# A transformer layer on one core: scaling of the second tokens on VectorE, low parts of the output projection on VectorE, first projections by bank

## The chip, the cores and the metric

The kernel runs on one core of a Trainium2 chip. The metric is the device time of one execution in microseconds (us), the median of several runs. TensorE multiplies matrices into PSUM banks, ScalarE, VectorE and GpSimd do the elementwise work, and SyncE issues the DMAs. Each of them works through its own queue in order; semaphores order them against each other.

## What is computed

One layer of an encoder over 2048 tokens of width 1024. What matters here is its first half:

```python
h = x * (1.0 + sc1) + sh1                       # sc1, sh1: a vector each, from c
proj = jnp.einsum('bsd,de->bse', h, w_in[l])    # u (512), q, k, v (512 each)
y_pool = pool_mixer(u, w_pool[l], pool_scale[l])
y_attn = chunked_attention(q, k, v, rel_bias[l])     # 8 heads, 9 chunks of 64 keys
y = jnp.einsum('bse,ed->bsd', jnp.concatenate([y_pool, y_attn], axis=-1), w_out[l])
x = layer_norm(ALPHA * x + (1.0 + g1) * y, ln1_g[l], ln1_b[l])
```

A squared-ReLU MLP (1024 to 4096 and back) and a second layer norm follow; no line of the change is in them.

## The kernel before

**Two parts per operand.** Each operand of a large product is kept as a high part (the value rounded to the matrix type, a copy on ScalarE) and a low part (value minus high part, a subtraction on VectorE or GpSimd). A product is three matmuls per 128 rows of the contraction: high by high, high by low, low by high. `split` (lines 57 to 59) issues the copy and the subtraction; its last argument is the engine of the subtraction.

**Stages.** The tokens go in two halves of 1024. The operand `hT` (128 partitions, high and low, 8 contraction blocks, 1024 tokens) lies in one buffer, which serves three things in turn: `h` of the first tokens, `h` of the second tokens, the output projection's weights.

- *Start* (to about 57 us): for each of 8 contraction blocks `k`, `chain0` and `fold0` make the two modulation vectors, `fold0` and `low0` make `hT` of that block, and `dense0(k)` (line 161) issues 18 matmuls: 3 passes by 3 projections (`FIRST`: A0 is q and k of head 0, V0 the values of heads 0 and 1, U0 a pooling group) by 2 halves of 512 tokens. They accumulate in six PSUM banks: A0 in the wide tile `S`, V0 in two of the three `d` banks, U0 in the third and in `pv`. The weights lie in the pool `ada`, which ends after this stage; the pool `attn` takes its place.
- *Attention with the other projections under it* (about 57 to 672 us): the loop over `units` (2 halves, 8 heads, 8 blocks of 128 queries) issues per unit `scores` (TensorE into `S`, line 600; VectorE adds the bias and takes the extremum, 607; ScalarE exponentiates, 609), `normalise` (VectorE reciprocal 614, GpSimd scaling 615), `transposes` (TensorE into `T`, 623), `probs` (ScalarE 631 and VectorE 632 out of `T`), and for every second unit `values` and `combine`. `S` and `T` have one buffer each. Between them `step` (line 446) lets the generator `dense` issue one projection matmul at a time, and calls `finish_evacs`, which moves each projection's evacuation (`evac`) on by one piece: ScalarE and VectorE take `q`, `k` or values out of their bank, values are transposed by TensorE (line 318).
- *Side work.* After every sixth matmul (every third for `wo_pieces(1)`) `dense` moves a side generator on by one piece. `h_pieces(tb)` (line 253) makes `h` of 512 second tokens, in 8 pieces: call `k` issues the scaling of piece `k` (GpSimd, 267), the high part of piece `k-1` (ScalarE, 269), the low part of piece `k-2` (VectorE, 271), and then a load. It runs twice, during the last blocks on the first tokens and the first block group on the second. `wo_pieces(n)` (line 663) does the like with the output projection's weights: load, copy, subtraction, eight pieces, twice. Both draw their raw tiles from `xr` (`xr_tile`, line 248), a ring of 4 buffers that the generator `extras` uses too: it loads `wout` (517), scales it on GpSimd (527) and stores it. `extras` pauses from unit 44 to unit 70 (line 727).

**The order around the change.** It is written out by hand (`manual_schedule`): each engine executes its instructions in the order in which Python issues them. The order of `pend` (line 362), from which `finish_evacs` takes one piece of each kind per call, is that of `FIRST`: A0, V0, U0. Weights of the projections are split by `split` on GpSimd (`hl`, line 59).

Of the kernel before, what the change touches and what calls it, by code (L numbers as in the profile page):

```python
# [11 lines left out]
ALU = mybir.AluOpType  # L12
# [12 lines left out]
def trunk_layer(ctx: ExitStack, tc: tile.TileContext, xT, x, wada1, wada2, vecs, rows, win, wfirst, wpT, wout,  # L25
                bias, w1, w2, out):
    nc = tc.nc
# [25 lines left out]
    mod1 = const.tile([128, 8, 2], F32, name="mod1")  # L53
# [3 lines left out]
    def split(hl_h, hl_l, src, low):  # L57
        nc.scalar.copy(hl_h, src)  # L58
        low.tensor_sub(hl_l, src, hl_h.bitcast(F32))  # L59
# [43 lines left out]
    FIRST = ("A0", "V0", "U0")  # L103
# [14 lines left out]
    hT = big.tile([128, 2, 8, 1024], F32R, name="hT", tag="big")  # L118
# [15 lines left out]
    def dbank():  # L134
        return pp.tile([128, 512], F32, name="d", tag="d", bufs=3)
# [4 lines left out]
    def narrow(w=512):  # L140
        return pr.tile([128, w], F32, name="pv", tag="pv", bufs=1)
# [3 lines left out]
    NF0 = len(FIRST)  # L145
    wf = ada.tile([128, 2, 8, NF0, 128], F32R, name="wf")
    s0 = wide("S")
    first = {(0, 0): s0[:, 0:512], (0, 1): s0[:, 512:1024], (1, 0): dbank(), (1, 1): dbank(), (2, 0): dbank(),
             (2, 1): narrow()}
# [9 lines left out]
        ld[k] = (wr, wa, xk)  # L159

    def dense0(k):
        for i, (a, b) in enumerate(((0, 0), (1, 0), (0, 1))):
            for c in range(NF0):
                for tb in range(2):
                    nc.tensor.matmul(first[c, tb], wf[:, a, k, c, :], hT[:, b, k, tb * 512:tb * 512 + 512],
                                     start=(k == 0 and i == 0), stop=(k == 7 and i == 2))

    acs = {}

# [36 lines left out]
    for k in range(8):  # L206
        if k < 4:
            load0(k + 4)
        if k == 4:
            st.dma_to(1)  # L210
        if k < 7:
            fold0(k + 1)
        if k < 6:
            chain0(k + 2)
        if k < 7:
            low0(k + 1)
        if k < 6:
            split0(k + 2)
        if k == 5:
            st.split_to(1)  # L220
        dense0(k)
# [20 lines left out]
    def flush():  # L242
        while later:
            later.pop(0)[1]()
# [3 lines left out]
    def xr_tile():  # L248
        while stores:
            stores.pop(0)()  # L250
        return ap.tile([128, 512], F32, name="xr", tag="xr", bufs=4)

    def h_pieces(tb):
        c0, cols = 1024 + tb * 512, slice(tb * 512, tb * 512 + 512)
        rs = {}

        def load(k):
            rs[k] = xr_tile()
            nc.sync.dma_start(rs[k], xT[k, :, c0:c0 + 512])

        for k in range(4):
            load(k)
        yield
        for k in range(10):
            if k < 8:
                r = rs[k]
                nc.gpsimd.tensor_scalar(r, r, mod1[:, k, 1:2], mod1[:, k, 0:1], op0=ALU.mult, op1=ALU.add)
            if 1 <= k < 9:
                nc.scalar.copy(hT[:, 0, k - 1, cols], rs[k - 1])
            if k >= 2:  # L270
                nc.vector.tensor_sub(hT[:, 1, k - 2, cols], rs.pop(k - 2), hT[:, 0, k - 2, cols].bitcast(F32))
                if k + 2 < 8:
                    load(k + 2)
            if k < 7 or k == 9:
                yield
# [3 lines left out]
    def alloc(hf, kind, idx):  # L279
        if kind == "A":  # L280
            Qt[hf, idx] = ap.tile([128, 1024], F32R, name="q", bufs=2)
            Kt[hf, idx] = kk = ap.tile([128, 2, 1536], F32R, name="k", bufs=2)
            if hf:
                for s in range(2):
                    nc.sync.dma_start(kk[64 * s:64 * s + 64, :, 0:512].bitcast(F32), kS[idx].bitcast(F32))
        elif kind == "V":
            Vt[hf, idx] = vv = ap.tile([128, 12, 2, 128], F32R, name="v", bufs=2)
            if hf:
                nc.sync.dma_start(vv[:, 0:4].bitcast(F32), vS[idx].bitcast(F32))
# [61 lines left out]
    def run(g):  # L351
        for _ in g:
            pass
# [4 lines left out]
    def both(c, name):  # L358
        for tb in range(2):
            yield from evac(0, name[0], int(name[1]), tb, first[c, tb], dbank)  # L360

    for c, name in enumerate(FIRST):
        alloc(0, name[0], int(name[1]))
        g = both(c, name)
        pend.append((g, (0, name), name[0]))
# [30 lines left out]
    def dense():  # L396
        w, open_, side = {}, [], iter(())
        for hf, name, tb in blocks():
# [11 lines left out]
            if (hf, name, tb) in ((0, "U1", 1), (1, "A0", 0), (1, "A0", 1), (1, "U0", 1)):  # L410
                run(side)
                side = iter(()) if (hf, name, tb) == (1, "A0", 1) else wo_pieces(0) if (hf, name) == (1, "U0") else h_pieces(hf)
                next(side, None)
# [15 lines left out]
            pend.append((evac(hf, kind, idx, tb, ps, dbank), (hf, name) if tb else None, kind))  # L429
        run(side)  # L430
        side = wo_pieces(1)
        next(side)
        for t in range(3):
# [229 lines left out]
    def wo_pieces(n):  # L663
        run(ex[0])
        run(ex[1])
        flush()
        cols = slice(n * 512, n * 512 + 512)
        rs = {}

        def load(k):  # L670
            rs[k] = xr_tile()
            nc.sync.dma_start(rs[k], woS[k, :, cols])

        for k in range(4):
            load(k)
        yield
        for k in range(8):
            r = rs.pop(k)
            split(hT[:, 0, k, cols], hT[:, 1, k, cols], r, nc.vector if k % 2 else nc.gpsimd)
            if k + 4 < 8:  # L680
                load(k + 4)
            yield
# [8 lines left out]
    for n in range(-LA, NU + 2):  # L691
        m = n + LA
        if m < NU:
            hf, h, i = units[m]
# [20 lines left out]
        if 2 <= n and n % 2 == 0:  # L715
            hf, h, i = units[n - 2]
# [641 lines left out]
```

## Time and profile before

| | |
|---|---|
| median of 3 runs | 2167.26 us (2165.09 to 2168.88) |
| the profiled execution's own time | 2166.34 us |
| its span, first to last instruction | 2164.6 us |
| mean granted clock of TensorE | 0.983 |
| busy: TensorE, VectorE, ScalarE, GpSimd | 95%, 61%, 46%, 20% |

A row of the timeline gives the start in us, the time from there to the end of the merged instructions, engine, line, operation, output tile and input tiles with shapes, the count, and in square brackets how long the engine had been idle and what released it. `SPq` and the like are queues of an engine, where DMAs are issued and semaphores awaited. PEld is the weight load of TensorE, which overlaps the matmuls.

### The profile page before, as it was taken

What the parts mean: (1) busy time and instruction counts of PE and PEld (TensorE: products, weight loads), DVE (VectorE), ACT (ScalarE), POOL (GpSimd) and SP (SyncE); (2) the same over time, 40 slices, a digit from 0 to 9 for tenths busy, and PEclk for the clock granted to TensorE, in tenths of its full rate; (3) what the DMA queues carried; (4) which work ended last, traced back from release to release, by engine and by line L of the source; (5) the groups of instructions that cost most, each with busy time, mean ns of one, the idle gap of its engine ahead of it and who ended that gap; (6) DMA issues with size and microseconds to landing.
All of it is one profiled execution on the core that took longest, in us unless ns stands there. A gap on an engine that the chain in (4) does not pass through costs nothing. (4 is left out here: it accounts for less than half of the span.)

```text
span 2164.6 us, 27212 instructions
## 1 busy us (share of the span) xinstructions
PE 2059.5 (95%) x9672; PEld 1696.2 (78%) x9672; DVE 1319.5 (61%) x1930; ACT 997.6 (46%) x1596; POOL 427.8 (20%) x474
## 2 busy tenths in 40 slices
PE   7999989999999988799999899999999999989997
PEld 6778878888887866578888688888778888878886
DVE  7555555556664453577766665666586448974448
ACT  4454555555553543445555655455444333243331
POOL 1535454553242000000000000000170004510002
PEclk9999999999999999899999999999999999999999
DMA  7444553444443666888787888887866556675552
GB/s 292 143 130 121 152 156 92 124 136 123 137 127 103 192 194 204 265 280 307 274 294 276 294 299 291 292 300 278 314 236 236 191 189 230 221 246 195 194 185 107
DMA packets 236457, 455.64 MB, mean 211 GB/s; under 512 B 19105, under 2 KB 69793, under 8 KB 234786
## 3 DMA queue, kind: packets, MB, share of 16 engines
q1 hardware_dynamic: 236322, 453.91, 62.8%
q8 instruction: 76, 1.25, 0.2%
q14 instruction: 59, 0.48, 0.1%
HBM read 294.45 MB, written 151.00 MB: 206 GB/s over the span
## 5 line engine op out<-in xcount | busy, mean ns | idle before, releaser
L960 PE MATMUL f<-h,hl 128*128 128x512 f32 x2688 | 627.4, 395 | 19.9 <-DVE h L59 7.5
L1246 PE MATMUL f<-sb,sa 128*128 128x512 f32 x2688 | 619.8, 393 | 10.2 <-DVE sb L59 9.6
L960 PEld LDWEIGHTS f<-h,hl 128*128 128x128 f32 x2688 | 508.9, 190 | 138.8 <-DVE h L59 8.6
L1246 PEld LDWEIGHTS f<-sb,sa 128*128 128x128 f32 x2688 | 506.6, 189 | 123.3 <-DVE sb L59 11.7
L418 PE MATMUL d<-hT,hl 128*128 128x512 f32 x1392 | 374.6, 401 | 1.9 <-ACT vt L313 1.9
L418 PEld LDWEIGHTS d<-hT,hl 128*128 128x128 f32 x1392 | 250.1, 190 | 42.5 <-ACT vt L313 2.3
L632 DVE TENSOR_TENSOR PT<-T,PT 128x640 fp32r<-128x640 f32 (+4 forms) x128 | 94.8, 741 | 218.4 <-ACT PT L631 216.4
L609 ACT ACTIVATE s<-s,m 128x640 f32<-128x640 f32 (+4 forms) x128 | 97.8, 764 | 222.0 <-DVE m L607 171.0
L382 PE MATMUL d<-hT,hl 128*128 128x512 f32 x696 | 174.7, 409 | 9.6 <-DVE xt L835 9.6
L382 PEld LDWEIGHTS d<-hT,hl 128*128 128x128 f32 x696 | 134.9, 197 | 39.7 <-issue 10.8
L982 ACT ACTIVATE g<-g 128x512 f32<-128x512 f32 x96 | 60.8, 633 | 212.6 <-DVE g L973 205.3
L59 DVE TENSOR_TENSOR sb<-hl,sb 128x1024 fp32r<-128x1024 f32 x67 | 96.6, 1442 | 84.4 <-ACT sb L58 83.8
L58 ACT CAST sb<-hl 128x1024 fp32r<-128x1024 f32 x67 | 70.1, 1046 | 163.0 <-PE f L1246 142.6
L615 POOL TENSOR_SCALAR s<-s,m 128x640 f32<-128x640 f32 (+4 forms) x128 | 96.6, 755 | 242.1 <-DVE m L614 199.7
L1287 POOL TENSOR_SCALAR ag<-ag 128x1024 f32<-128x1024 f32 x1 | 1.3, 1340 | 680.7 <-DMA ag<-in_rows_dram 680.7
L59 DVE TENSOR_TENSOR hl<-wsum,hl 128x1024 fp32r<-128x1024 f32 x62 | 75.9, 1225 | 92.1 <-ACT hl L58 92.1
L59 DVE TENSOR_TENSOR sb<-raw,sb 128x1024 fp32r<-128x1024 f32 x45 | 70.1, 1557 | 63.2 <-ACT sb L58 62.9
L1215 POOL TENSOR_SCALAR zv<-zv 128x1 f32<-128x1 f32 x16 | 18.4, 1149 | 448.2 <-DVE zv L1214 448.2
L600 PE MATMUL S<-k,q 128*128 128x320 f32 (+1 forms) x448 | 92.0, 321 | 12.8 <-DVE m L607 12.8
L623 PE MATMUL T<-ident,s 128*128 128x128 f32 x560 | 83.9, 277 | 18.0 <-DVE PT L632 13.2
L623 PEld LDWEIGHTS T<-ident,s 128*128 128x128 f32 x560 | 67.3, 142 | 41.8 <-POOL hl L59 13.6
L58 ACT CAST sb<-raw 128x1024 fp32r<-128x1024 f32 x45 | 47.1, 1046 | 114.5 <-PE f L1246 92.1
(172 smaller groups left out, 2626.0 us busy)
## 6 DMA issues: line engine op xcount, KB each, us to landing
fS<-g SPq DMA_DIRECT2D x224, 256.0 KB, 3.6
hl<-fS SPq DMA_DIRECT2D x67, 512.0 KB, 4.9
hl<-tS SPq DMA_DIRECT2D x67, 512.0 KB, 5.0
w<-in_w_dram SPq DMA_DIRECT2D x46, 512.0 KB, 4.1
raw<-fS SPq DMA_DIRECT2D x45, 512.0 KB, 4.8
raw<-tS SPq DMA_DIRECT2D x45, 512.0 KB, 4.9
raw<-in_w_dram SPq DMA_DIRECT2D x34, 512.0 KB, 5.3
tS<-tw SPq DMA_DIRECT2D x64, 256.0 KB, 4.5
```

What stands on the lines that cost most here:

```text
L58: nc.scalar.copy(hl_h, src)
L59: low.tensor_sub(hl_l, src, hl_h.bitcast(F32))
L382: nc.tensor.matmul(ps, yc[:, a, k, :], hT[:, b, k, cols], start=(k == 0 and i == 0), stop=(k == 7 and i == 2))
L418: nc.tensor.matmul(ps, w[name][:, a, k, :], hT[:, b, k, tb * 512:tb * 512 + 512], start=(n == 0), stop=(n == 23))
L600: nc.tensor.matmul(S[:, 512 * p:512 * p + wp], q[:, i * 128:i * 128 + 128], k[:, a, k0 + p * wp:k0 + p * wp + wp], start=(a == 0), stop=(a ...
L609: nc.scalar.activation(s[:, 0:w], s[:, 0:w], AF.Exp, bias=m[:, 0:1], scale=-1.0, accum_out=m[:, 1:2])
L615: nc.gpsimd.tensor_scalar(s[:, 0:nk * 128], s[:, 0:nk * 128], m[:, 1:2], 1.0, op0=ALU.mult, op1=ALU.mult)
L623: nc.tensor.transpose(t[:, j * 128:j * 128 + 128], s[:, j * 128:j * 128 + 128], ident)
L632: nc.vector.tensor_sub(ol, src, oh.bitcast(F32))
L960: nc.tensor.matmul(ps, w[:, p, c:c + 128], h[:, q, k, :], start=first and k == 0 and (p, q) == (0, 0), stop=k == 3 and p == 1, skip_group_ ...
L982: nc.scalar.activation(o, o, AF.Relu)
L1246: nc.tensor.matmul(bank, f, w, start=start, stop=stop, skip_group_check=True)
```

## The change

Four edits. `dense0`: for the last contraction block (`k == 7`) the 18 matmuls go bank by bank, V0's two banks first, then A0's, then U0's, with the three passes of a bank in a row; for the others nothing changes. The evacuations of the first projections stand in `pend` (and their tiles are allocated) in the order V0, A0, U0. In `h_pieces` the scaling goes from GpSimd to VectorE. In `wo_pieces` all low parts are made by VectorE; before, the even ones were made by GpSimd.

```diff
     def dense0(k):
-        for i, (a, b) in enumerate(((0, 0), (1, 0), (0, 1))):
-            for c in range(NF0):
-                for tb in range(2):
-                    nc.tensor.matmul(first[c, tb], wf[:, a, k, c, :], hT[:, b, k, tb * 512:tb * 512 + 512],
-                                     start=(k == 0 and i == 0), stop=(k == 7 and i == 2))
+        passes = ((0, 0), (1, 0), (0, 1))
+        order = [(i, c, tb) for i in range(3) for c in range(NF0) for tb in range(2)]
+        if k == 7:
+
+            order = [(i, c, tb) for c in (1, 0, 2) for tb in range(2) for i in range(3)]
+        for i, c, tb in order:
+            a, b = passes[i]
+            nc.tensor.matmul(first[c, tb], wf[:, a, k, c, :], hT[:, b, k, tb * 512:tb * 512 + 512],
+                             start=(k == 0 and i == 0), stop=(k == 7 and i == 2))
...
-                nc.gpsimd.tensor_scalar(r, r, mod1[:, k, 1:2], mod1[:, k, 0:1], op0=ALU.mult, op1=ALU.add)
+                nc.vector.tensor_scalar(r, r, mod1[:, k, 1:2], mod1[:, k, 0:1], op0=ALU.mult, op1=ALU.add)
             if 1 <= k < 9:
                 nc.scalar.copy(hT[:, 0, k - 1, cols], rs[k - 1])
             if k >= 2:
...
-    for c, name in enumerate(FIRST):
+    for c, name in sorted(enumerate(FIRST), key=lambda v: (1, 0, 2)[v[0]]):
         alloc(0, name[0], int(name[1]))
...
-            split(hT[:, 0, k, cols], hT[:, 1, k, cols], r, nc.vector if k % 2 else nc.gpsimd)
+            split(hT[:, 0, k, cols], hT[:, 1, k, cols], r, nc.vector)
```

## Rows read from the trace of the kernel before

**Rows 1.** Waits of TensorE, 52 to 700 us: us in total, times, longest.
```profile
PE T L623 <- DVE PT L632: 13.2, 17, 2.4
PE S L600 <- DVE m L607: 12.8, 12, 2.2
```

**Rows 2.** Stretches: length; busy PE, PEld, DVE, ACT, POOL; clock; DMA share; GB/s.
```profile
284.00:334.00 50.00, 39.63 (x196) 32.53 (x195) 27.77 (x61) 27.84 (x58) 30.65 (x36) 0.93 0.56 161
302.00:308.00 6.00, 4.63 (x22) 4.25 (x22) 3.49 (x7) 2.37 (x4) 3.63 (x5) 0.72 0.59 163
618.00:662.00 44.00, 39.75 (x214) 33.64 (x213) 25.80 (x49) 25.14 (x50) 24.30 (x28) 0.92 0.39 124
```

**Rows 3.** Timeline, all engines, end of the start stage.
```profile
56.46 0.40 PE L165 MATMUL pv<-hT,wf 128*128 128x512 f32 x1
56.89 0.33 SPq L580 DMA_DIRECT2D bias<-in_bias_dram  x1
56.89 0.59 ACT L296 ACTIVATE q<-S 64x512 fp32r<-64x512 f32 x1 [5.79 <-PE pv L165]
...
58.10 0.58 ACT L313 COPY vt<-d 128x512 f32<-128x512 f32 x1
58.11 0.69 DVE L299 SCALAR_TENSOR_TENSOR q<-S,q 64x512 fp32r<-64x512 f32 x1 [5.42 <-ACT k L297]
...
58.74 1.43 PE L418 MATMUL d<-hT,hl 128*128 128x512 f32 x5 [1.88 <-ACT vt L313]
...
59.53 0.59 ACT L296 ACTIVATE q<-S 64x512 fp32r<-64x512 f32 x1 [0.36 <-DVE k L302]
...
61.22 0.59 ACT L313 COPY vt<-d 128x512 f32<-128x512 f32 x1
...
61.87 0.66 PE L318 MATMUL d<-ident,vt 128*128 128x128 f32 x4
```

**Rows 4.** Timeline of TensorE, two of its waits in the first side stage.
```profile
297.91 0.86 PE L600 MATMUL S<-k,q 128*128 128x320 f32 x4 [2.20 <-DVE m L607]
...
303.37 0.88 PE L623 MATMUL T<-ident,s 128*128 128x128 f32 x5 [3.00 <-POOL hl L59]
```

**Rows 5.** Timeline of SyncE's queue: third, fourth and fifth load of the second tokens.
```profile
275.96 0.33 SPq L259 DMA_DIRECT2D xr<-in_xT_dram  x1
287.64 0.33 SPq L259 DMA_DIRECT2D xr<-in_xT_dram  x1
289.94 0.34 SPq L259 DMA_DIRECT2D xr<-in_xT_dram  x1
```

**Rows 6.** Timeline of VectorE: first low part, and the first operation after the last.
```profile
286.94 0.67 DVE L271 TENSOR_TENSOR hT<-xr,hT 128x512 fp32r<-128x512 f32 x1
...
333.88 0.28 DVE L632 TENSOR_TENSOR PT<-T,PT 128x128 fp32r<-128x128 f32 x1
```

**Rows 7.** Users of tile xr, 260 to 400 us: ns min/median/max, first and last start us.
```profile
L267 POOL TENSOR_SCALAR xr<-xr,mod x16: 762/768/1435, 285.0 to 331.8; 128x512 f32<-128x512 f32 x16
L271 DVE TENSOR_TENSOR hT<-xr,hT x16: 665/692/1151, 286.9 to 333.3; 128x512 fp32r<-128x512 f32 x16
L517 SPq DMA_DIRECT2D xr<-in_wout_dram x2: 424/546/667, 259.4 to 398.0; - x2
L527 POOL TENSOR_TENSOR xr<-xr,xa x2: 1301/1304/1308, 259.9 to 398.5; 128x512 f32<-128x512 f32 x2
```

**Rows 8.** Line 259, the 16 loads of the second tokens: issue to landing.
```profile
DMA to landing us min/median/max: 2.9/4.4/6.0
```

**Rows 9.** Users of tile xr in the whole span, as in rows 7.
```profile
L484 DVE TENSOR_SCALAR xa<-xr,cs x6: 469/478/498, 85.5 to 547.5; 128x512 f32<-128x512 f32 x6
L59 POOL TENSOR_TENSOR hT<-xr,hT x8: 1262/1295/1302, 621.9 to 653.8; 128x512 fp32r<-128x512 f32 x8
L59 DVE TENSOR_TENSOR hT<-xr,hT x8: 684/710/1344, 626.0 to 656.8; 128x512 fp32r<-128x512 f32 x8
```

**Rows 10.** Waits of ScalarE, 284 to 334 us, as in rows 1.
```profile
ACT hT L269 <- POOL xr L267: 14.0, 9, 3.3
```

## The prediction, made before the change was run

> **What bounds the kernel now.** I read the page first: TensorE is busy 95% of the span, so a change can only pay where TensorE stands still. The waits of TensorE over the attention stage come next [rows 1]: nearly all of its idle time there ends with VectorE freeing one of two single PSUM tiles, `S` (line 607) or `T` (line 632). VectorE's place in time therefore counts in this stage, not its load. The stretches show where: in 284 to 334 us, where `h` of the second tokens is made, TensorE works 39.6 of 50 us, and after its longest waits it was granted the lower of its two levels for a while, 0.72 in the mean of 302 to 308 [rows 2]. In 618 to 662, the stage of `wo_pieces`, it works 39.8 of 44. The third place touched is the end of the start stage.
>
> **Part 1, start stage.** Two edits, one chain. Making V0's banks complete first lets nothing start earlier: the first instruction of ScalarE and the bias load of SyncE, which has nothing to do with TensorE, both start at 56.89, right behind the last matmul of `dense0` (56.46 + 0.40) [rows 3]. Whatever first writes into the new pool waits for the last reader of the old one, and that last matmul stays where it was. The price of the order is nothing: its third matmul of block 7 now needs the low part that the thirteenth needed, and that is ready by then (a margin of some 0.3 us in the timeline, an estimate).
>
> What counts is the order V0, A0, U0 on ScalarE. TensorE now waits for the third copy, `vt`, from 56.86 to 58.74 [rows 3]. With `vt` first it starts behind one copy: 56.89 + 0.58 + 0.05 = 57.52, a gain of 1.2. But A0's two copies move back by the length of `vt`, 0.5 (a full copy is followed by the next after about 0.48). VectorE's subtraction at 58.11 waits for them, the copy of A0's second half at 59.53 waits for VectorE, and in ScalarE's queue the second `vt` copy (61.22) stands behind that; the transposes at 61.87 wait for it [rows 3]. All of this moves by 0.5, so TensorE meets the transposes at about 62.35. The stall at the front is won and given back further down: **+0.5 us**, with bounds of -1.2 (the chain over A0 has slack that I don't see) and +0.7.
>
> **Part 2, scaling of the second tokens.** Sixteen scalings leave GpSimd (0.77 each) and go to VectorE. The nearest row for the price there is line 484, the same kind of operation and shape: 0.48 [rows 9]. By the sums it is cheap: 16 x 0.48 = 7.7 us on an engine that is idle for 22 of 50 [rows 2]. What decides is the place in the queue. Call `k` issues the scaling of piece `k` and behind it the low part of piece `k-2`, now both on VectorE.
>
> How many raw tiles are there? The ring has four, but one tile of `wout` that was loaded at 259.4 is scaled only at 398.5, when `extras` goes on [rows 7]; it holds a buffer through the whole stage. So three are left, and the trace shows it: the third load goes out at 275.96, the fourth only at 287.64 [rows 5], 0.03 behind the end of the first low part (286.94 + 0.67) [rows 6]; the fifth follows the second low part likewise, and so on. Load `k` waits for low part `k-3`. Before, that was harmless to VectorE: a scaling that waited for its load stood in GpSimd's queue, and low parts `k-2` and `k-1` went ahead, so that up to three loads were on their way.
>
> After the change the scaling of piece `k` stands in VectorE's queue **in front of** low part `k-2`. It waits for load `k`, which left only when low part `k-3`, the one just before, was done. One load is under way at a time, and VectorE stands still for its whole latency. What is queued behind it: lines 607 and 632, which free `S` and `T`, so TensorE waits too. Load `k+1` in SyncE's queue waits for low part `k-2`, with the stores and key copies between.
>
> One cycle is landing + scaling + low part + hand-overs. A landing takes 2.9 to 6.0, median 4.4 [rows 8]. Loads travel with less company when they go one at a time, so I take 3.6, nearer the low end. Scaling 0.48, low part 0.68, three hand-overs about 0.1 in all: 3.6 + 0.48 + 0.68 + 0.1 = 4.86. TensorE's work between two calls is some ten matmuls at 39.63 / 196 = 0.20, 2 us [rows 2], so it is hidden under the cycle and not the other way round.
>
> - First piece with a wait: the fourth load leaves at 288.6 instead of 287.64, since two of the first three scalings (0.48 each) now stand in front of the first low part.
> - Five pieces (`k` = 3 to 7): 5 x 4.86 = 24.3, so 312.9.
> - Two last low parts 1.3, overlapping with the first load of the next 512 tokens; that load, three scalings, the first low part and about 4 us of evacuations and attention work that stand between them (six operations at the 0.69 of the one in [rows 3]): 3.6 + 1.4 + 0.7 + 4.1 = 9.8, so 322.7.
> - Five pieces again: 347.0; two last low parts: 348.3.
>
> The operation behind the last low part started at 333.88 [rows 6]: **+14.4 us**. Eleven landings stand in this sum: with 2.9 for each it is 7.7 less, +6.7; with 4.4 it is 8.8 more, +23.2. TensorE then comes out of a long stretch of waits at the lower level: 6 us at 0.72 instead of 1.00 [rows 2] cost 1.7, so **+1.5**, 0 to 2.
>
> A word on the price of a load: the Trainium skill ("DMA: Bandwidth & Descriptors", section on the anatomy of one DMA) gives 2.0 us fixed plus bytes over 436 GB/s, for 256 KB an estimate of 2.6 us; by it the shift would be 11.0 less, +3.4. No load of line 259 landed as fast; the shortest took 2.9 [rows 8], so the trace is used.
>
> **Part 3, low parts of the output projection.** Eight subtractions leave GpSimd (1.295) and cost VectorE 0.71 [rows 9], 5.7 us over 44 in which it is idle for 18 [rows 2]. No load is waited for in VectorE's queue here, only ScalarE's copy just before. For: the low parts end earlier, so buffers come free 0.6 earlier, and VectorE's own operations, up to 1.3 where GpSimd works beside them, get shorter. Against: a subtraction that waits for its copy now stands ahead of lines 607 and 632, up to eight times. TensorE's idle time there is 4.25 in all [rows 2]; half of it won is -2, and eight delays of 0.3 are +2.4. I take **+0.5**.
>
> **Sum.** 0.5 + 14.4 + 1.5 + 0.5 = 16.9 on the profiled execution's 2166.3: 2183.2. That execution lies 0.9 below the median, so I give **2184 us**, 0.8% slower. Ends: 6.7 + 0 - 1.2 - 2 = +3.5, or 2171; 23.2 + 2 + 0.7 + 2.4 = +28.3, or 2196.
>
> **Rivals.**
>
> *VectorE gets to each scaling after its data have landed* (faster). Then the stage loses what it now suffers from GpSimd: ScalarE waits 14.0 us for scalings [rows 10], the wait of 3.00 at 303.37 and that of 2.20 at 297.91 follow from that and from late stores [rows 4]. TensorE's 10.4 idle us in 284 to 334 would shrink to a few: -10, so 2157. It holds from the point where load `k` is issued two calls ahead of scaling `k`, which needs a fourth buffer. Against it stand [rows 5, 7]. Here belongs the Trainium skill's rule ("GPSIMD Engine Reference", section 4.1 Engine selection): elementwise work on a tile belongs on VectorE, not GpSimd. The durations agree (1.295 against 0.71) [rows 9]; whether that turns into time hangs on the queue. Chance 0.11.
>
> *One side each way* (no change). The fourth buffer is free for one of the two times 512 tokens: that one gains half of the 10, -5, the other loses half of the forecast, +7, with the rest some +3, or 2170 at most and 2167 with landings of 2.9. It decides from the point where a tile comes back to the ring between 288 and 323. Only the two operations of [rows 7] touch the held tile in that time, at its start and behind its end, which speaks against it. Chance 0.09.
>
> *The start stage alone does what it is meant to*: -1.2 instead of +0.5, inside the range of the forecast.
>
> **How the numbers follow.** Forecast 0.80, the rivals 0.11 and 0.09. A measurement of this kernel can tell about 0.2%, 4.3 us, from no change. Faster: 0.11 + 0.02 = 0.13. Same: 0.07 from the second rival, little from the forecast's low end: 0.08. Slower: 0.79. The range runs from 2166, taking in half of the second rival, to 2196: 0.95 of 0.80 and 0.05 are 0.81.
>
> **What would show it.** In the profile after: VectorE at line 267 with idle time before it that ends with the DMA into `xr`, ten times, some 30 us in all, and none at GpSimd; loads of line 259 leaving one by one, each just behind a low part, about 4.9 apart; TensorE idle 25 us or more in the stage, released by VectorE. For part 1: the first matmul of line 418 at 57.5, and the second group of transposes later than 61.9, not earlier. For part 3: the waits of 618 to 662 within 2 us of now. The prediction is wrong if scalings on VectorE show no DMA wait, or if VectorE's order isn't the order of issue.

## The result, and the profile after

The changed kernel takes 2183.75 us in the median of 6 runs (2178.73 to 2186.69) against 2166.43 of 6 runs of the kernel before (2163.09 to 2170.88): the ratio is 1.0076, 95% interval 1.0060 to 1.0092. The profiled execution took 2184.12, its span is 2182.3; in spans it lies 17.7 us above the profiled one of before. A line number of after is 4 higher than that of before: the load of `h_pieces` is line 263, the scaling 271, the copy 273, the low part 275; lines 604, 611, 627 and 636 are 600, 607, 623 and 632.

VectorE's waits in the stage where `h` of the second tokens is made, 280 to 365 us (total us, times, longest):

```profile
DVE xr L271 <- DMA xr<-in_xT_dram: 27.1, 11, 3.7
DVE PT L636 <- ACT PT L635: 9.4, 7, 2.0
```

The first row stands nowhere in the profile of before. There the scaling waited in GpSimd's queue, and VectorE had no wait for these loads. VectorE's timeline shows where these 27.1 us lie (start, duration, what ran, in brackets the idle time ahead of it and what ended it):

```profile
293.68 0.55 DVE L271 TENSOR_SCALAR xr<-xr,mod 128x512 f32<-128x512 f32 x1 [2.86 <-DMA xr<-in_xT_dram]
294.14 0.68 DVE L275 TENSOR_TENSOR hT<-xr,hT 128x512 fp32r<-128x512 f32 x1
...
298.25 1.36 DVE L271 TENSOR_SCALAR xr<-xr,mod 128x512 f32<-128x512 f32 x1 [2.61 <-DMA xr<-in_xT_dram]
299.54 1.75 DVE L275 TENSOR_TENSOR hT<-xr,hT 128x512 fp32r<-128x512 f32 x1
...
304.41 0.55 DVE L271 TENSOR_SCALAR xr<-xr,mod 128x512 f32<-128x512 f32 x1 [2.33 <-DMA xr<-in_xT_dram]
...
350.45 0.29 DVE L636 TENSOR_TENSOR PT<-T,PT 128x128 fp32r<-128x128 f32 x1
```

Load, wait, scaling, low part, and only then the next load: SyncE's queue sends it 0.08 us behind the end of the low part at 294.14 (294.14 + 0.68 = 294.82).

```profile
294.90 0.34 SPq L263 DMA_DIRECT2D xr<-in_xT_dram  x1
```

The last row of VectorE's fence is the operation behind the last low part. It stood at 333.88 before [rows 6], so it comes 16.57 us later. The time from issue to landing of the 16 loads has a shorter median than before, 3.7 for 4.4 [rows 8]; the ends hardly differ. The DMA share of the stage fell from 0.56 [rows 2] to 0.44 (below), which fits the prediction's guess that loads with less company land sooner, but no run tests that by itself. Issue to landing:

```profile
DMA to landing us min/median/max: 3.0/3.7/6.2
```

For TensorE, these stretches answer [rows 2] (length; busy PE, PEld, DVE, ACT, POOL; clock; DMA share; GB/s):

```profile
284.00:350.00 66.00, 46.90 (x200) 37.07 (x199) 35.81 (x77) 27.00 (x58) 16.15 (x20) 0.79 0.44 122
300.00:305.00 5.00, 2.37 (x7) 1.58 (x7) 2.67 (x5) 0.27 (x1) 0.74 (x1) 0.60 0.18 52
305.00:311.00 6.00, 4.65 (x13) 3.51 (x14) 3.27 (x7) 3.16 (x6) 2.08 (x2) 0.50 0.17 44
...
350.00:356.00 6.00, 6.00 (x35) 5.10 (x35) 3.80 (x11) 3.16 (x7) 2.47 (x5) 1.00 0.21 46
```

TensorE is idle for 19.1 of 66 us, where it was idle for 10.4 of 50. All of it ends with VectorE at the two lines that free `T` and `S` (waits of TensorE, 280 to 352 us):

```profile
PE T L627 <- DVE PT L636: 12.0, 5, 3.8
PE S L604 <- DVE m L611: 7.1, 3, 2.9
```

TensorE also ran slower: 305 to 311 lies wholly at the lower of its two clock levels (0.50 of 2.4 GHz, that is 1.2), after a stretch in which it had worked 2.37 of 5 us. At 350 to 356 it is back at the full clock and has no idle time.

At the end of the start stage (TensorE and ScalarE), to be read beside [rows 3]:

```profile
56.49 0.86 PE L169 MATMUL pv<-hT,wf 128*128 128x512 f32 x3
...
57.39 0.59 ACT L317 COPY vt<-d 128x512 f32<-128x512 f32 x1 [5.79 <-PE pv L169]
...
58.03 1.43 PE L422 MATMUL d<-hT,hl 128*128 128x512 f32 x5 [0.68 <-ACT vt L317]
...
60.52 0.59 ACT L300 ACTIVATE q<-S 64x512 fp32r<-64x512 f32 x1 [0.85 <-DVE k L306]
...
62.21 0.59 ACT L317 COPY vt<-d 128x512 f32<-128x512 f32 x1
```

The last matmul of `dense0` ends at 57.35 (before: 56.86). The first dense matmul now waits 0.68 us instead of 1.88, but the second transposes stood at 62.86 in this run, 5.51 behind that end, where it was 61.87 - 56.86 = 5.01.

In the stage of `wo_pieces`, TensorE waited for 0.85 + 2.92 + 0.20 + 1.56 = 5.5 us, against 4.25 [rows 2]:

```profile
657.41 0.85 PE L604 MATMUL S<-k,q 128*128 128x320 f32 x4 [0.85 <-DVE m L611]
...
662.56 1.09 PE L627 MATMUL T<-ident,s 128*128 128x128 f32 x5 [2.92 <-DVE PT L636]
...
673.27 0.74 PE L627 MATMUL T<-ident,s 128*128 128x128 f32 x5 [0.20 <-DVE PT L636]
...
679.52 0.74 PE L627 MATMUL T<-ident,s 128*128 128x128 f32 x5 [1.56 <-DVE PT L636]
```

### The profile page after: what moved, and what is told of

Its sections match the earlier page's. It is cut to its first block, busy times and chain, and to the rows that moved or that the text cites. A ratio compares the mean times of both kernels' runs of the same rounds, so it can differ in the third digit from the quotient of the medians.

```text
span 2182.3 us, 27221 instructions
## 1 busy us (share of the span) xinstructions
PE 2067.6 (95%) x9672; PEld 1700.4 (78%) x9672; DVE 1330.4 (61%) x1954; ACT 998.0 (46%) x1596; POOL 401.9 (18%) x450
## 5 line engine op out<-in xcount | busy, mean ns | idle before, releaser
L604 PEld LDWEIGHTS S<-k,q 128*128 128x128 f32 x448 | 75.4, 191 | 38.4 <-DVE m L611 24.9
```

The source lines that it names most:

```text
L604: nc.tensor.matmul(S[:, 512 * p:512 * p + wp], q[:, i * 128:i * 128 + 128], k[:, a, k0 + p * wp:k0 + p * wp + wp], start=(a == 0), stop=(a ...
```

## Experiments

Theory: the loss comes from part 2, by the queue. A scaling that waits for its load stands on VectorE ahead of the low part that lets the next load go, and since one of four raw tiles is held by a `wout` tile, one load at a time is under way. Rivals: the amount of work that VectorE got (7.7 and 5.7 us); late loads alone, whatever the queue; the start stage. Ratios are against runs of the kernel before on the same chip, whose medians were 2164.8 us (part 2 alone, the held tile, the queue), 2166.6 (part 1, part 3, both mends) and 2166.7 (the others).

**Part 2 alone.**

```diff
-                nc.gpsimd.tensor_scalar(r, r, mod1[:, k, 1:2], mod1[:, k, 0:1], op0=ALU.mult, op1=ALU.add)
+                nc.vector.tensor_scalar(r, r, mod1[:, k, 1:2], mod1[:, k, 0:1], op0=ALU.mult, op1=ALU.add)
```

> The kernel before with part 2 alone: the sixteen scalings of h_pieces on VectorE, nothing else. The theory (one load under way at a time, because a scaling that waits for its load stands ahead of the low part that lets the next load go): the operation behind the last low part moves from 333.9 to some 349.5 us, VectorE waits for the load ten or eleven times, some 27 us in all, and the whole is +15 to +17 us against before (some 2183). The rival (the loss comes from the three parts together, or from the start stage): under +8 us.

Measured: 2180.63 us, ratio 1.0062 (1.0050 to 1.0074), which is +13.4 us; the medians differ by 15.8. VectorE's wait in 280 to 365 us:

```profile
DVE xr L267 <- DMA xr<-in_xT_dram: 25.9, 11, 3.5
```

The operation behind the last low part, in VectorE's timeline:

```profile
347.65 0.28 DVE L632 TENSOR_TENSOR PT<-T,PT 128x128 fp32r<-128x128 f32 x1
```

It moves by 13.8 us against 333.88 [rows 6], some 2 less than I expected. The whole is by the ratio a little below the +15 to +17 that I expected, by the medians within it; either way it is most of the change's loss, and the rival that needs all three parts falls.

**The held tile given back, scalings on VectorE as changed.** The pause of `extras` ends two units sooner, and two empty jobs take the place of the two in which the tile was loaded and held; all other jobs stay in their units.

```diff
+                    if (k, n) == (5, 0):
+                        jobs += [((lambda: None), (lambda: None))] * 2
                     jobs += wo_job(k, n, box)
...
-    LA, EXTRA = 3, (44, 70, 118)
+    LA, EXTRA = 3, (44, 68, 118)
```

> The changed kernel, with the wout tile that is held through the pause not loaded before the pause: two empty jobs stand ahead of that tile's job, and the pause ends two units sooner, so that all else comes in the old order. The ring of four raw tiles then has four for h_pieces, and load k waits for low part k-4 instead of k-3. If the held tile is what makes one load go at a time, two are under way, a cycle of 4.9 us serves two pieces, VectorE's wait for loads falls from 27 us to under 10, and the whole loses most of what it was slower: 2166 to 2172. If the loss comes from the scaling's place or its load on VectorE in itself, it stays above 2178.

Measured: 2165.2 us, ratio 0.9994 (0.9982 to 1.0006). That is 0.8 below the range that I expected, 2166 to 2172. Nothing else of the change was taken back, and its whole loss is gone. VectorE's wait for loads in 280 to 365 us:

```profile
DVE xr L271 <- DMA xr<-in_xT_dram: 7.0, 5, 4.3
```

The low parts (count, ns min/median/max, first and last start):

```profile
L275 DVE TENSOR_TENSOR hT<-xr,hT x16: 677/684/1754, 286.7 to 329.2; 128x512 fp32r<-128x512 f32 x16
```

27.1 us became 7.0, and the last low part starts at 329.2 instead of 349.8. The work on VectorE is the same as in the changed kernel, so the rival of the amount falls.

**The same tile given back to the kernel before.** The same edit of `extras`, in the kernel before.

> The same fourth raw tile given to the kernel before, whose scalings stand in GpSimd's queue. By the theory VectorE never waited for a load there, but ScalarE waited 14.0 us for scalings: with loads leaving one piece sooner the stage gets up to 5 us shorter, 2161 to 2167. The rival that GpSimd itself bounds the stage gives no change, within 2 us.

Measured: 2162.9 us, ratio 0.9982 (0.9970 to 0.9993). The last low part starts at 326.0, 7.3 sooner than the 333.3 of [rows 7]; 2.2 of these the run had gained ahead of the stage (first low part at 284.7 instead of 286.9). The profiled run was also the fastest of this kernel's twelve, 2155.13. ScalarE's wait for scalings falls from 14.0 [rows 10] to this (280 to 365 us):

```profile
ACT hT L269 <- POOL xr L267: 8.5, 8, 2.0
```

So late loads cost something in the kernel before, too: some 4 us of the whole. But the missing tile costs the changed kernel 18 (ratios 1.0076 and 0.9994).

**The queue turned round, the tile still held.** In each call the low part goes ahead of the scaling.

```diff
-            if k < 8:
-                r = rs[k]
-                nc.vector.tensor_scalar(r, r, mod1[:, k, 1:2], mod1[:, k, 0:1], op0=ALU.mult, op1=ALU.add)
             if 1 <= k < 9:
                 nc.scalar.copy(hT[:, 0, k - 1, cols], rs[k - 1])
             if k >= 2:
                 nc.vector.tensor_sub(hT[:, 1, k - 2, cols], rs.pop(k - 2), hT[:, 0, k - 2, cols].bitcast(F32))
                 if k + 2 < 8:
                     load(k + 2)
+            if k < 8:
+                r = rs[k]
+                nc.vector.tensor_scalar(r, r, mod1[:, k, 1:2], mod1[:, k, 0:1], op0=ALU.mult, op1=ALU.add)
```

> The changed kernel with one thing turned round: in each call of h_pieces the low part of piece k-2 (and the load that follows it) is issued ahead of the scaling of piece k. The held tile stays held, the work on VectorE is the same. If the order in VectorE's queue is the cause, two loads are under way at a time and low parts no longer stand behind a scaling's wait: VectorE's wait for loads falls by half or more and the whole is within 5 us of before, 2164 to 2172. If it is the amount of work on VectorE, or the late loads alone, nothing changes against 2184.

Measured: 2169.51 us, ratio 1.0022 (1.0010 to 1.0033). Here the low part is line 272 and the scaling 277. VectorE's wait for loads in 280 to 365 us:

```profile
DVE xr L277 <- DMA xr<-in_xT_dram: 12.5, 8, 4.1
```

The low parts, as above:

```profile
L272 DVE TENSOR_TENSOR hT<-xr,hT x16: 667/682/935, 288.7 to 336.9; 128x512 fp32r<-128x512 f32 x16
```

Same tiles, same work, only the order of two instructions in one queue: VectorE's wait is halved, the last low part starts 12.9 us sooner than in the changed kernel, and some two thirds of the loss are gone. The edit also sends each load off without waiting for a scaling, so by itself it doesn't part late loads from the queue; but the kernel before has the same three tiles, with the scalings on GpSimd, and loses only some 4 us by them. Late loads alone don't explain the loss; the order in VectorE's queue does, and three tiles are what makes it bite.

**Part 1 alone** (the two edits of the start stage as in the diff ahead of the prediction).

> The kernel before with part 1 alone (block 7 of dense0 bank by bank, V0's banks and evacuation first). The theory: the first dense matmul starts some 0.6 us behind the end of dense0's last matmul instead of 1.9, and the second group of transposes 5.5 us behind it instead of 5.0, since the chain over A0 is pushed back by one copy; the whole +0.5 us, which the times can't tell from nothing. The rival (the edit gains its 1.2 us): second transposes at 3.8 us behind, and whole -1.2.

Measured: 2165.11 us, ratio 0.9998 (0.9987 to 1.0010), no difference that can be told. The trace of TensorE tells more:

```profile
56.08 0.86 PE L169 MATMUL pv<-hT,wf 128*128 128x512 f32 x3
...
57.62 1.43 PE L422 MATMUL d<-hT,hl 128*128 128x512 f32 x5 [0.68 <-ACT vt L317]
59.31 0.66 PE L322 MATMUL d<-ident,vt 128*128 128x128 f32 x4 [0.27 <-ACT u L333]
...
62.44 0.66 PE L322 MATMUL d<-ident,vt 128*128 128x128 f32 x4 [1.08 <-ACT vt L317]
```

Three waits of 0.68 + 0.27 + 1.08 = 2.03 took the place of one of 1.88; with matmuls in another order between them the second transposes stand 62.44 - 56.94 = 5.50 behind `dense0`, 0.5 later than before. What is won at the front is given back.

**Of part 1 only the order of the banks** (the edit against part 1 alone).

```diff
-    for c, name in sorted(enumerate(FIRST), key=lambda v: (1, 0, 2)[v[0]]):
+    for c, name in enumerate(FIRST):
```

> Of part 1 only the order of the matmuls in block 7; the evacuations in the order A0, V0, U0 as before. The theory: the first copy out of the banks still starts behind the very last matmul of dense0 (within 0.1 us of its end), because it writes into a pool that lies where the old pool was; first dense matmul 1.9 us behind, second transposes 5.0 us behind, as before. The rival (banks that are complete are read at once): the first copy starts 3 us or so ahead of the end of dense0.

Measured: 2163.47 us in one run, too few to judge the time by. Timeline, several engines:

```profile
56.82 0.87 PE L169 MATMUL pv<-hT,wf 128*128 128x512 f32 x3
...
57.72 0.33 SPq L584 DMA_DIRECT2D bias<-in_bias_dram  x1
57.72 0.59 ACT L300 ACTIVATE q<-S 64x512 fp32r<-64x512 f32 x1 [5.79 <-PE pv L169]
...
59.57 1.43 PE L422 MATMUL d<-hT,hl 128*128 128x512 f32 x5 [1.88 <-ACT vt L317]
```

A0's banks and V0's were complete before the last three matmuls, into `pv`. Still the first copy, and a load of SyncE that reads no bank at all, start 0.03 us behind the very last matmul (57.69). Finishing banks early buys nothing while the first write into the new pool waits for the old pool's last reader. The second transposes stand at 62.70, 5.01 behind, as before.

**Part 3 alone** (all low parts of `wo_pieces` on VectorE).

> The kernel before with part 3 alone: all low parts of wo_pieces on VectorE. The theory: +0.5 us, from -2 to +2.4; TensorE's waits in 618 to 662 us go from GpSimd's low parts over to VectorE's line 632, with a sum within 2 us of before. By the difference between the changed kernel and part 2 alone (2183.8 and 2180.6) parts 1 and 3 together would be worth some +2.

Measured: 2168.64 us, ratio 1.0013 (0.9999 to 1.0028): +2.8 by the ratio, with an interval that just reaches nothing. TensorE's waits in 620 to 720 us:

```profile
PE T L623 <- DVE PT L632: 6.3, 4, 2.9
PE S L600 <- DVE m L607: 1.6, 2, 1.3
```

7.9 us against 4.2 before, and all of it still behind VectorE. I had expected it within 2 us of before, and the +2.8 lies above the bound of +2.4. VectorE's wait for ScalarE's copies, 615 to 700 us, with part 3 alone (first row) and in the kernel before (second):

```profile
DVE hT L59 <- ACT hT L58: 9.6, 8, 1.5
...
DVE hT L59 <- ACT hT L58: 10.7, 6, 2.8
```

**Part 3 with its low parts one call later**, so that the subtraction doesn't wait for ScalarE's copy (the edit against part 3 alone).

```diff
-        for k in range(8):
-            r = rs.pop(k)
-            split(hT[:, 0, k, cols], hT[:, 1, k, cols], r, nc.vector)
-            if k + 4 < 8:
-                load(k + 4)
-            yield
+        for k in range(9):
+            if k < 8:
+                nc.scalar.copy(hT[:, 0, k, cols], rs[k])
+            if k >= 1:
+                nc.vector.tensor_sub(hT[:, 1, k - 1, cols], rs.pop(k - 1), hT[:, 0, k - 1, cols].bitcast(F32))
+                if k + 3 < 8:
+                    load(k + 3)
+            if k != 7:
+                yield
```

> Part 3 alone as before, but the low part of a piece is issued one call later than its copy, so that it doesn't wait for ScalarE's copy in VectorE's queue. With part 3 alone VectorE waited 9.6 us for these copies (eight times) and TensorE's waits in 618 to 662 us were 7.9 us against 4.2 before. If the low part's wait ahead of lines 607 and 632 is the cause: VectorE's wait for the copies falls under 2 us, TensorE's waits back to 4.2 or below, and the whole is 2162 to 2167 (before 2166). If the extra 5.7 us of work on VectorE are the cause, TensorE's waits stay at 7 or more and the whole at 2168.

Measured: 2166.92 us, ratio 1.0002 (0.9991 to 1.0013). VectorE's wait for the copies in 615 to 700 us:

```profile
DVE hT L681 <- ACT hT L679: 3.7, 5, 0.9
```

TensorE's waits in 618 to 662 us:

```profile
PE T L623 <- DVE PT L632: 4.9, 3, 2.9
PE S L600 <- DVE m L607: 0.2, 1, 0.2
```

VectorE's wait fell from 9.6 to 3.7, not under 2, and TensorE's from 7.9 to 5.1, not to 4.2. The work on VectorE is the same, so waiting less for copies helps TensorE. It doesn't show that this wait is what part 3 added: the kernel before has as much of it, 10.7 us, and its TensorE waits are 4.2. That part 3 costs TensorE something is seen in every profile: at lines 600 and 623 (by their numbers in the kernel before) it waits in this stage 3.8 to 4.8 us in the seven kernels without part 3, 5.5 to 8.1 in the five with it, 5.1 in the two with the late low parts. How much of it is the subtractions' work and how much their place in the queue stays open, and the intervals of the times overlap.

**The changed kernel with both mends** (low part first and tile given back).

> The changed kernel with both mends: the low part ahead of the scaling, and the held wout tile not held. Load k then waits for low part k-4 and is issued two calls ahead of scaling k, the point from which the first rival of the prediction holds (-10 against before). If that price was right: VectorE's waits for loads under 3 us, 2155 to 2159. If TensorE's idle time in the stage has another source than the scalings (VectorE's waits for ScalarE's copies at lines 632 and 607): 2161 to 2166, no better than either mend with GpSimd.

Measured: 2165.83 us, ratio 0.9998 (0.9984 to 1.0012). VectorE's wait for loads is down to 5.1 us, two times, and the last low part starts at 327.8. The waits are not under 3 us as that price would have it, and the -10 of the prediction's first rival is not there, although its loads now leave one tile sooner; the next runs tell what is left of its condition.

**Part 2 alone with both mends, and with even pieces back on GpSimd.**

> Part 2 alone with both mends: scalings on VectorE behind the low part, fourth raw tile; start stage and wo_pieces as before. It tells what moving the scalings is worth once no load is waited for. In the run with all three parts the last low part of h started at 327.8 us, with scalings on GpSimd and the fourth tile at 326.0: so no gain from the move, 2162 to 2167. If the move is worth what the prediction's first rival said: 2155 to 2159.

> As the run before it, but even pieces are scaled on GpSimd and odd ones on VectorE. If VectorE's queue and GpSimd's queue each carry too much in this stage, the halves end earlier than either alone: last low part of h before 325 us, 2158 to 2163. If the stage is set by something else (ScalarE's copies at line 631 with the attention's work), it ends within 1.5 us of 326.

Measured: 2163.54 us, ratio 0.9989 (0.9977 to 1.0000), and 2164.41, ratio 0.9990 (0.9975 to 1.0005); the last low parts start at 330.3 and 326.7. From the first low part to the last it is 42.0 and 40.1 us, with scalings on GpSimd and the fourth tile 41.3: no gain that can be told from moving them (0.9982 there). In both kernels lines 602, 609, 625 and 634 are 600, 607, 623 and 632 of before. One wait carries half of what TensorE still loses there (timeline of part 2 alone with both mends; SyncE, VectorE, TensorE):

```profile
302.55 2.59 SPq L259 DMA_DIRECT2D xr<-in_xT_dram  x4
...
308.59 1.11 DVE L273 TENSOR_SCALAR xr<-xr,mod 128x512 f32<-128x512 f32 x1 [4.22 <-DMA xr<-in_xT_dram]
...
310.58 0.74 PE L625 MATMUL T<-ident,s 128*128 128x128 f32 x5 [4.13 <-DVE PT L634]
```

The four loads of the second 512 tokens go out at once, and the first scaling is issued only one call behind them: on VectorE it stops the queue for a whole landing again. TensorE's waits in 280 to 350 us are 6.2 at line 634 and 2.2 at line 609; without this one 4.3 are left, all behind VectorE. With the even pieces on GpSimd VectorE never waits for a load in this stage, and TensorE still waits 7.4 us (280 to 350):

```profile
PE T L625 <- DVE PT L634: 4.0, 3, 1.5
PE S L602 <- DVE m L609: 3.4, 3, 2.0
```

**The kernel before with the fourth tile and the late low parts of `wo_pieces`.**

> The kernel before with the fourth raw tile (2162.9 before on another chip, TensorE's waits in 618 to 662 us 3.9 us) and the late low parts of wo_pieces on VectorE. By the theory both gains add: 2159 to 2164, faster than both kernels. By the rival (work on VectorE) it is 2165 or more.

Measured: 2162.72 us, ratio 0.9986 (0.9973 to 1.0000); the last low part starts at 328.4. Within the range, but the two edits show no sum: the fourth tile alone gave 0.9982. So the best ratio measured is that of the kernel before with only the held tile given back, 4 us or 0.18% faster than before, about the bound of what can be told; the intervals of the other kernels with the fourth tile overlap with it.

## Why the prediction held

**Part 2's mechanism** stands as it was put, step by step. Three tiles, one load under way, VectorE idle for the landing: giving back the tile and turning the queue round each take most of it away alone (27.1 us of waiting become 7.0 and 12.5). The cycle was given as 4.86; from the end of the first low part (289.61) to that of the sixth (314.92) it is 25.31 / 5 = 5.06, in the second 512 tokens (325.36 to 349.33) 23.97 / 5 = 4.79. Both sets of tokens go one load at a time, so the second rival, one side each way, falls. Landings of 3.6 were taken, near the low end of [rows 8], because loads would go one at a time; the median became 3.7. A scaling took 0.55, not 0.48. The bridge between the two sets of tokens was 9.8, measured 10.4. The Trainium skill's price that the prediction quotes ("DMA: Bandwidth & Descriptors", section on the anatomy of one DMA) is given there for transfers that GpSimd issues, and these loads are issued by SyncE; as an estimate it is 2.6 us. In the changed kernel no load landed in less than 3.0, so the trace was the better source.

The stage as a whole: 16.57, less the 0.99 by which the start stage had already moved, is 15.6, against +14.4. Eleven waits for loads instead of ten (the eleventh is the first scaling of the second 512, whose landing stood in the sum but not in the list of what to look for), 27.1 us instead of some 30. An error of 1.2 is also about what the stage moves by itself: from the first low part to the last it took 44.5 to 46.4 us in the five kernels whose code there is that of before.

**The clock** was mis-placed: 1.5 us were to come after the stage. The profile shows the full clock from 350 on, so that term is 0. The lower level lies inside the stage, 0.79 in its mean: 200 matmuls took 46.90 us there, where 196 took 39.63 before. At the pace of before they would have taken some 40.4 (an estimate), and the idle time would be 25.6 us instead of 19.1, near the 25 that I named. So the slower matmuls seem to fill time in which TensorE would otherwise have waited for VectorE; no run parts the two. That the two errors, 1.5 too much here and 1.2 too little in the stage, nearly cancel is luck, and so is 2183.75 against my 2184.

**Part 1** came out to the tenth where it can be seen, in the trace: first dense matmul 0.68 behind `dense0` (predicted 57.52 - 56.86 = 0.66), second transposes 0.5 later. The other 0.5 of the changed kernel's shift is not the change's: `dense0` ended at 56.86 before, 57.35 in the changed kernel, 56.94 with part 1 alone and 57.69 with the order of the banks alone: it moves from run to run by more than that, and not with the edits: in all profiles it lies between 56.1 and 57.8 without the new order of the banks, between 56.3 and 57.7 with it.

**Part 3** was sized too small. +0.5 was the guess, from -2 to +2.4. Alone it cost TensorE 7.9 - 4.2 = 3.7 us of waits in the profiled run and the whole 2.8 us by the ratio, with an interval that reaches nothing; in the changed kernel 5.5 - 4.25 = 1.3. What failed is the gain set against the price: low parts of 0.69 us instead of 1.295 show no gain for TensorE in any profile, while in the five kernels with part 3 TensorE waits 1.3 to 3.8 us more than before, where +2.4 was taken as the upper bound.

**The sum.** In profiled spans: 0.5 of start stage, 0.5 from run to run ahead of it, 15.6 of the stage and 1.3 of `wo_pieces` are 17.9, against 17.7. That it closes so well is luck: the first matmul of the MLP stands at 888.4 us against 873.8 (line 964, 960 before), 14.6 later, and the other 3.1 arise behind it, where the change has no line. In ratios of the medians: part 2 +0.62%, part 3 +0.13%, part 1 -0.02%, together +0.73%, against +0.76%, each with an interval of 0.1% or more to both sides. No interplay is needed.

**The first rival** had the wrong price. With the fourth tile VectorE no longer loses most of the landings, and with every second piece on GpSimd it loses none, but of the -10 only 4 us were to be had with scalings on GpSimd (0.9982), and no more with them on VectorE (0.9989). TensorE's waits in 280 to 350 us were 10.9 before, 8.2 with the fourth tile alone, 8.4 with the scalings on VectorE in addition, and 7.4 with every second one there. The price took nearly all idle time of the stage for the doing of scalings and late loads; of the 8.2, 5.3 stand behind VectorE at the two lines that free `S` and `T`, and remain. The Trainium skill's rule that elementwise work belongs on VectorE ("GPSIMD Engine Reference", section 4.1 Engine selection) holds for the duration, 0.55 against 0.77 us for a scaling here, which is less than the factor of about two that it gives for operations with two inputs; for the time of the kernel, no run shows a gain from it, with or without the fourth tile.

## What to carry to other kernels

Before moving an operation to a faster engine, ask what it waits for and what stands behind it in the new queue: 0.2 us per operation were saved, and 27 us of waiting for loads arose where TensorE feels them. Here the instruction that frees a buffer stood behind one that waits for a load into the same ring, and three buffers worked like one; issue the freeing instruction first, and look for tiles that a paused job holds. And a stage whose first write waits for the last reader of an old pool can't be started early by finishing parts of the old one sooner.

## What the runs showed of the hardware that I had not expected

VectorE's operations on the same shapes stretched more beside GpSimd than the 1.34 of [rows 9] had shown. In the changed kernel a scaling took 1.36 us at 298.25 and the low part behind it 1.75, against 0.55 and 0.68 some 5 us before. GpSimd's timeline in that time:

```profile
298.26 1.06 POOL L340 TENSOR_TENSOR ws<-ws 128x525 f32<-128x525 f32 x1
299.28 1.46 POOL L59 TENSOR_TENSOR hl<-raw,hl 128x512 fp32r<-128x512 f32 x1
```

Both of VectorE's operations lie under these two; at 293.68 GpSimd was idle. It is the same in all fourteen profiles: of the operations on `xr` tiles that VectorE ran while GpSimd was idle, no scaling took more than 0.55 us and no low part more than 0.70; the longest beside a GpSimd operation took 1.37 and 1.75. What the two engines contend for, no run here tells apart.
